# A decoder layer in one core: the projections after q, k, v with activations instead of weights as the stationary operand

## The chip, the core and the metric

One core of a Trainium2 chip runs the whole layer in one launch. TensorE (PE) multiplies matrices and writes to PSUM; VectorE (DVE), ScalarE (ACT) and GpSimd (POOL) work on tiles; SyncE (SP) issues DMAs. The metric is the device time in microseconds of the core. The kernel before takes 1522.69 us (median of three runs, 1522.31 to 1523.57).

## The reference

For 256 tokens of width 2048, in float32, with P the weights' columns of each part:

```
u = rmsnorm(x)
q,k,v,z | beta,decay | qb,kb,vb | gate_a,gate_b = u @ w_in
y_a = gated_deltanet(conv(q,k,v), z, beta, decay)     # 8 heads of 128
y_b = block attention(qb, kb, vb)                     # 8 heads of 128
mix = sigmoid(gate_a) * (y_a @ w_gdn) + sigmoid(gate_b) * (y_b @ w_moba)
h   = x + mix @ w_out
u   = rmsnorm(h)
out = h + (silu(u @ w_gate) * (u @ w_up)) @ w_down    # w_gate, w_up: 2048 x 5632
```

## The kernel before, in words

All weights stand in DRAM in the order of their use as 504 units of 128 partitions x 1024 float32 (512 KB). Each is split into `whi` (rounded to the matmul's fp32r type, by ACT, L67) and `wlo` (the rest, by DVE, L68). Activations are kept split in the same way, as a high part of 256 tokens and a low part of 256 tokens in one row of 512. A product is the sum hi*hi + hi*lo + lo*hi, in one of two forms:

- `fm_jobs` (feature-major, L149): a 128x128 piece of the weights is the stationary operand. `whi` meets all 512 columns of the activations (L169), `wlo` the 256 high ones (L170). A unit is 8 such pairs, 16 matmuls with 6144 moving columns in all. The output stands features x tokens, in two halves that have to be added (`evac`, ACT L279 and DVE L280).
- `tm_job` (token-major): a 128x128 piece of the activations is stationary, and 512 columns of weights move past it: high x `whi` (L189), high x `wlo` (L190), low x `whi` (L191). A unit is 4 such triples, 12 matmuls with 6144 moving columns as well. The output stands tokens x features in one piece.

Units 0 to 111 are q, k, v of the convolution (fm), z and qb, kb, vb (tm). The other 392 units are all fm before the change: gates and branches 96, w_out 32, gate and up 176, down 88.

`Weights.get` runs through the units: it asks for loads ahead (DMAs on SP's queue, 1 MB chunks of two units, three buffers), splits up to three units ahead into four buffers, and hands one unit to PE. The small work of the attention parts is a set of generators (`chains`), of which a job advances one step every so many matmuls (`tick`); what is put into `late` runs whole at the next tick. Instructions then stand on each engine's queue in an order that the tile framework chooses and are executed in that order; an instruction waits for its operands by semaphores, and what stands behind it waits too. Two PSUM tiles of two banks (`mm`) hold the jobs' sums, four single banks (`aux`) all else.

At the start `x_part` (L230) loads x in four chunks and the first weights, and two fm jobs run together. In g = 0 of the first attention part a 16x16 solve loads `lb` (1 MB, broadcast out of a DRAM scratch, issued by ACT) and works on it on DVE (L485, L486).

Of the kernel before, what the change touches and what calls it, by code (L numbers as in the profile page):

```python
# [16 lines left out]
P = 128  # L17
# [16 lines left out]
SPLIT_AHEAD = 3  # L34
TICK = 8


class Weights:
# [3 lines left out]
    def __init__(self, nc, pool, src):  # L42
        self.nc, self.pool, self.src = nc, pool, src
        self.n = 2 * src.shape[0]
        self.raw, self.parts = {}, {}

    def load(self, c):
        if c in self.raw or 2 * c >= self.n:
            return
        t, src = self.pool.tile([P, 2, 1024], F32, name="wraw", tag="wraw", bufs=3), self.src[c]  # L50
        if c == 0:
            self.first = [lambda: self.nc.sync.dma_start(t[:, 0, :512], src[:, 0, :512]),
                          lambda: self.nc.sync.dma_start(t[:, 0, 512:], src[:, 0, 512:]),
                          lambda: self.nc.sync.dma_start(t[:, 1], src[:, 1])]
# [25 lines left out]
def layer(ctx: ExitStack, tc: tile.TileContext, xT, xtok, params, consts, relt, w_bd, w, out):  # L80
# [35 lines left out]
    warm = small("warm", [2])  # L116
    nc.scalar.activation(warm, ones[:, :2], AF.Tanh)

# [30 lines left out]
    def fm_jobs(act, nk, m, before=None, apart=False):  # L149

        get = act if callable(act) else lambda kc: act[:, kc]
        if apart:
            pss = [[aux.tile([P, 512], F32, name="psh", tag="aux") for _ in range(2)]]
            halves = pss
        else:
            pss = [mm.tile([P, 2, 512], F32, name="ps", tag="mm") for _ in range(m)]
            halves = [[ps[:, j] for j in range(2)] for ps in pss]
        for k0 in range(0, nk, 4):  # L160
            if before:
                before(k0)
            for ps in halves:
                hi, lo = W.get(cursor[0])
                cursor[0] += 1
                for j in range(2):
                    for kc in range(k0, k0 + 4):
                        sl = slice((kc % 4) * 256 + j * P, (kc % 4) * 256 + (j + 1) * P)
                        nc.tensor.matmul(ps[j], hi[:, sl], get(kc), start=kc == 0, stop=False)  # L169
                        nc.tensor.matmul(ps[j][:, :T], lo[:, sl], get(kc)[:, :T], start=False, stop=kc == nk - 1)  # L170
# [7 lines left out]
    def tm_job(act, nk):  # L178

        ps = mm.tile([P, NT, 512], F32, name="ps", tag="mm")  # L180
        for kc in range(nk):
# [4 lines left out]
            for n in range(NT):  # L186
                ah = act[:, kc, n * P:(n + 1) * P]
                al = act[:, kc, T + n * P:T + (n + 1) * P]
# [7 lines left out]
    def token_scale(name, ssq, rows=None):  # L196


        rb, r = small(name + "b", [T]), small(name, [NT])

        def steps():
            total = ssq
            if rows is not None:
                with tc.issue_after(W.last_hi.ins):
                    for n in range(NT):
                        nc.scalar.activation(rows[:, n], rows[:, n], AF.Square, accum_out=ssq[:, n:n + 1])
            else:
                p = aux.tile([P, 512], F32, name="pss", tag="aux")
                for n in range(NT):
                    nc.tensor.matmul(p[:, 2 * n:2 * n + 2], ssq[:, n * P:(n + 1) * P], ones[:, :2], start=True,  # L210
                                     stop=True)
                total = p[:, :2 * NT].rearrange("p (n j) -> p n j", j=2)[:, :, 0]
            nc.vector.tensor_copy(r, rsqrt(name + "r", total, 1.0 / DM))
            yield
            p2 = aux.tile([P, 512], F32, name="pbc", tag="aux")
            for n in range(NT):
                nc.tensor.transpose(p2[:, n * P:(n + 1) * P], r[:, n:n + 1].to_broadcast([P, P]), ident)
            nc.vector.tensor_copy(rb, p2[:, :T])

        return r, rb, steps()  # L220
# [3 lines left out]
    rsum = small("xssq", [NT])  # L224
    xrow = acts.tile([P, NT, DM], F32, name="xrow", tag="actB")
    with tc.tile_pool(name="xin", bufs=4) as xin:
        xcs = {}

        def x_part(k0):
            xc = xcs[k0] = xin.tile([P, 4, T], F32, name="xc", tag="xc")  # L230
            W.load(k0 // 4)
            if k0 == 0:
                for i in range(2):
                    W.first[i]()
                    nc.sync.dma_start(xc[:, 2 * i:2 * i + 2], xT[:, 2 * i:2 * i + 2])
                W.first[2]()
            else:
                nc.sync.dma_start(xc, xT[:, k0:k0 + 4])
            if k0 == 4:
                nc.sync.dma_start(ident, consts[:, :P])  # L240
            if k0 == 8:
                nc.sync.dma_start(par, params)
            if k0 == KM - 4:
                nc.sync.dma_start(xrow, xtok)
            for k in range(4):
                kc = k0 + k
                nc.scalar.activation(aT[:, kc, :T], xc[:, k], AF.Copy, scale=wmix[:, kc:kc + 1])
                nc.vector.scalar_tensor_tensor(aT[:, kc, T:], xc[:, k], wmix[:, kc:kc + 1],  # L248
# [123 lines left out]
    def gdn_project(g):  # L372
# [8 lines left out]
        held = [evac(ps, "cu", md, "md", 6) for ps in first] if g == 0 else []  # L381
        for i in range(len(held), len(dsts)):
            u = evac(fm_job(aT, KM), "cu", md, "md", 6)
            if held:
                drain(1)
                nc.vector.tensor_scalar(r1h, r1, 0.5, None, op0=ALU.mult)
# [334 lines left out]
    def gated(yT, dst):  # L721
        s = evac(fm_job(aT, KM), "gt", md, "md", 6)
        nc.gpsimd.tensor_mul(s, s, bcm(r1b, 2))
        nc.scalar.activation(s, s, AF.Tanh, scale=0.5)
        b = evac(fm_job(yT, H), "br", md, "md", 6)
        nc.vector.scalar_tensor_tensor(dst, s, 1.0, b, op0=ALU.add, op1=ALU.mult)
# [4 lines left out]
    for j in range(KM // 2):  # L731
        m = s2.tile([P, 2, T], F32, name="mix", tag="t2", bufs=14)
        gated(yaT, m)
        mix.append(m)
# [5 lines left out]
    for j in range(KM // 2):  # L740
        m = md.tile([P, 2, T], F32, name="mixb", tag="md", bufs=6)
        gated(ybT, m)
        nc.gpsimd.tensor_add(m, m, mix[j])
        hi = mixT[:, 2 * j:2 * j + 2, :T]
        nc.scalar.activation(hi, m, AF.Copy, scale=0.5)
        nc.vector.scalar_tensor_tensor(mixT[:, 2 * j:2 * j + 2, T:], m, 0.5, hi.bitcast(F32),
                                       op0=ALU.mult, op1=ALU.subtract)


    hT = acts.tile([P, KM, T], F32, name="hT", tag="actB")  # L750
    uT = acts.tile([P, KM, 512], F32R, name="uT", tag="actA")
    hsq = small("hsq", [T])
    for j in range(KM // 2):
        xr = md.tile([P, 2, T], F32, name="xr", tag="md", bufs=6)
        nc.sync.dma_start(xr, xT[:, 2 * j:2 * j + 2])
        ps = fm_job(mixT, KM)
        hj = hT[:, 2 * j:2 * j + 2]
        nc.vector.tensor_add(hj, ps[:, :, T:], xr)
        nc.vector.tensor_add(hj, ps[:, :, :T], hj)
        for i in range(2):  # L760
            kc = 2 * j + i
            nc.scalar.activation(uT[:, kc, :T], hT[:, kc], AF.Copy, scale=wffn[:, kc:kc + 1])
            nc.vector.scalar_tensor_tensor(uT[:, kc, T:], hT[:, kc], wffn[:, kc:kc + 1],
                                           uT[:, kc, :T].bitcast(F32), op0=ALU.mult, op1=ALU.subtract)
        sq = md.tile([P, 2, T], F32, name="hq", tag="md", bufs=6)
        nc.scalar.activation(sq, hj, AF.Square)
        if j == 0:
            nc.gpsimd.tensor_add(hsq, sq[:, 0], sq[:, 1])
        else:
            nc.gpsimd.tensor_add(sq[:, 0], sq[:, 0], sq[:, 1])  # L770
            nc.gpsimd.tensor_add(hsq, hsq, sq[:, 0])
    low_stage.close()
    mid.close()
    r2, r2b, scale_steps = token_scale("r2", hsq)
    r2bh = small("r2bh", [T])
    chains.append(scale_steps)
# [134 lines left out]
```

## Time and profile before

| | |
|---|---|
| median of three runs | 1522.69 us |
| the profiled execution | 1520.97 us |
| its span, first to last instruction | 1519.2 us |
| granted TensorE clock, mean | 0.999 |
| PE busy | 1496.4 us (99%) |
| DVE, ACT, POOL busy | 937.1, 712.3, 161.7 us |
| DMA | 277.95 MB, 183 GB/s on average |

Times in the rows are microseconds from the start of the span, unless marked ns. A matmul's own duration overlaps that of its neighbours; what a stream of them costs is the distance from start to start. L numbers are lines of the kernel. PEld is PE's loading of stationary operands, which runs beside the matmuls.

### The profile page before, as it was taken

The numbers are of one execution on the slowest core, as the hardware profiler recorded it, in microseconds if no ns is written. First come the engines' busy times: TensorE is split into PE (matmuls) and PEld (weight loads), VectorE is DVE, ScalarE is ACT, GpSimd is POOL, SyncE is SP. The second block draws the span as 40 slices with busy tenths as digits, with TensorE's granted clock in tenths as the row PEclk, the third lists the DMA queues.
The fourth block names the chain that finished last, engine by engine and source line by source line (L and its number), as shares of the span: only waits on it lengthen the run. The fifth ranks groups of instructions, "written<-read, shape, count | busy, mean of one in ns | idle before, by whom it ended". The sixth has DMA issues, their size and how long they took to land.

```text
span 1519.2 us, 21248 instructions
## 1 busy us (share of the span) xinstructions
PE 1496.4 (99%) x8586; PEld 1291.0 (85%) x8586; DVE 937.1 (62%) x1231; ACT 712.3 (47%) x1008; POOL 161.7 (11%) x125
## 2 busy tenths in 40 slices
PE   7999899999999999999999999999999999999999
PEld 5888778887888888888888888888888888888887
DVE  5878867866775566666665555555555655444443
ACT  5644445445454444554544444444444444333332
POOL 0003002301100111111221111111111110000000
PEclk9999999999999999999999999999999999999999
DMA  8453634643435555556655555555455555555552
GB/s 322 167 198 137 194 112 166 181 182 112 181 129 191 194 195 189 185 186 219 220 188 177 190 194 181 182 192 190 177 189 194 182 181 192 199 190 193 201 190 80
DMA packets 41841, 277.95 MB, mean 183 GB/s; under 512 B 4752, under 2 KB 5648, under 8 KB 9232
## 3 DMA queue, kind: packets, MB, share of 16 engines
q1 hardware_dynamic: 41040, 274.25, 50.9%
q10 hardware_dynamic: 704, 2.36, 0.7%
q8 instruction: 67, 1.10, 0.3%
q14 instruction: 30, 0.25, 0.0%
HBM read 274.36 MB, written 2.23 MB: 182 GB/s over the span
## 4 chain that ended last, share of the span: by engine, by line
PE 91%; DVE 4%; DMA 2%; ACT 1%; POOL 1%; issue 1%; SPq 0%; ACTq 0%; POOLq 0%
PE ps L169 49%; PE ps L170 25%; PE ps L189 4%; PE ps L191 4%; PE ps L190 3%; DMA wraw<-in_w 2%; PE psh L169 1%; DVE wlo L68 1%; DVE cacc L365 1%; PE psh L170 1%; ACT whi L67 0%; PE pO L699 0%; PE pU L566 0%; PE pO L574 0%; PE pb L296 0%
## 5 line engine op out<-in xcount | busy, mean ns | idle before, releaser
L68 DVE TENSOR_TENSOR wlo<-wraw,whi 128x1024 fp32r<-128x1024 f32 (+1 forms) x505 | 639.5, 1268 | 449.7 <-ACT whi L67 449.0
L67 ACT CAST whi<-wraw 128x1024 fp32r<-128x1024 f32 (+1 forms) x505 | 528.3, 1049 | 632.9 <-PE ps L169 518.6
L169 PE MATMUL ps<-uT,whi 128*128 128x512 f32 x1408 | 497.7, 399 | 0.0
L170 PE MATMUL ps<-uT,wlo 128*128 128x256 f32 x1408 | 395.4, 281 | 0.0
L169 PE MATMUL ps<-aT,whi 128*128 128x512 f32 x896 | 319.2, 398 | 9.7 <-DVE aT L248 7.9
L169 PEld LDWEIGHTS ps<-uT,whi 128*128 128x128 f32 x1408 | 264.5, 188 | 66.0
L170 PEld LDWEIGHTS ps<-uT,wlo 128*128 128x128 f32 x1408 | 266.0, 189 | 0.0
L170 PE MATMUL ps<-aT,wlo 128*128 128x256 f32 x896 | 253.7, 283 | 7.5 <-DVE wlo L68 7.4
L169 PEld LDWEIGHTS ps<-aT,whi 128*128 128x128 f32 x896 | 169.5, 189 | 48.7 <-DVE aT L248 8.9
L170 PEld LDWEIGHTS ps<-aT,wlo 128*128 128x128 f32 x896 | 171.0, 191 | 9.8 <-DVE wlo L68 9.6
L169 PE MATMUL ps<-high,whi 128*128 128x512 f32 x504 | 178.4, 399 | 0.0
L170 PE MATMUL ps<-high,wlo 128*128 128x256 f32 x504 | 141.6, 281 | 0.0
L169 PEld LDWEIGHTS ps<-high,whi 128*128 128x128 f32 x504 | 94.7, 188 | 23.6
L189 PE MATMUL ps<-whi,aT 128*128 128x512 f32 x256 | 102.0, 398 | 0.0
L191 PE MATMUL ps<-whi,aT 128*128 128x512 f32 x256 | 101.2, 395 | 0.0
L190 PE MATMUL ps<-wlo,aT 128*128 128x512 f32 x256 | 100.5, 392 | 0.0
L170 PEld LDWEIGHTS ps<-high,wlo 128*128 128x128 f32 x504 | 95.2, 189 | 0.0
L169 PE MATMUL ps<-mixT,whi 128*128 128x512 f32 x256 | 88.8, 391 | 0.0
L170 PE MATMUL ps<-mixT,wlo 128*128 128x256 f32 x256 | 71.7, 280 | 0.0
L169 PEld LDWEIGHTS ps<-mixT,whi 128*128 128x128 f32 x256 | 47.9, 187 | 10.5
L191 PEld LDWEIGHTS ps<-whi,aT 128*128 128x128 f32 x256 | 48.1, 188 | 9.7
L190 PEld LDWEIGHTS ps<-wlo,aT 128*128 128x128 f32 x256 | 48.1, 188 | 9.2
(335 smaller groups left out, 1456.2 us busy)
## 6 DMA issues: line engine op xcount, KB each, us to landing
wraw<-in_w SPq DMA_DIRECT2D x251, 1024.0 KB, 4.8
xrow<-in_xtok SPq DMA_DIRECT2D x1, 2048.0 KB, 13.8
lb<-dm ACTq DMA_DIRECT2D x2, 1024.0 KB
xr<-in_xT SPq DMA_DIRECT2D x8, 256.0 KB, 5.3
out<-fo SPq DMA_DIRECT2D x7, 256.0 KB, 2.8
xc<-in_xT SPq DMA_DIRECT2D x3, 512.0 KB, 10.9
bias<-in_relt SPq DMA_DIRECT2D x4, 256.0 KB, 5.1
wraw<-in_w SPq DMA_DIRECT2D x2, 256.0 KB, 3.9
```

The costliest lines, as they stand in the source:

```text
L67: self.last_hi = self.nc.scalar.copy(hi[:, f], raw[:, f])
L68: self.last_lo = self.nc.vector.tensor_sub(lo[:, f], raw[:, f], hi[:, f].bitcast(F32))
L169: nc.tensor.matmul(ps[j], hi[:, sl], get(kc), start=kc == 0, stop=False)
L170: nc.tensor.matmul(ps[j][:, :T], lo[:, sl], get(kc)[:, :T], start=False, stop=kc == nk - 1)
L189: nc.tensor.matmul(ps[:, n], ah, hi[:, sl], start=kc == 0, stop=False)
L190: nc.tensor.matmul(ps[:, n], ah, lo[:, sl], start=False, stop=False)
L191: nc.tensor.matmul(ps[:, n], al, hi[:, sl], start=False, stop=kc == nk - 1)
L365: nc.vector.scalar_tensor_tensor(acc[:, j, d:], u[:, j, :T - d], w[:, 3 - d:4 - d], acc[:, j, d:], op0=ALU.mult, op1=ALU.add)
```

## The change

The 392 units after qb, kb, vb become `tm_job`s; `gated`, the w_out loop and the FFN loops are written anew for token-major outputs. Norm factors are then per partition, so they go into the activation's scale or a scalar operand, and the POOL multiplications by a broadcast row go. Where the next product needs the result as its stationary operand (the mix, h, and the FFN's hidden values), PE turns it: `turn` puts four 128x128 transposes into an `aux` bank and ACT and DVE split them from there. Two turns (one per 128 tokens) run at the first tick of the next job, after 24 of its matmuls; there are 4 pairs for the mix, 4 for h and 11 for the hidden values. The sum of squares of h comes from ACT's accumulation by rows, not from a matmul with ones (`pss`) and a broadcast by PE (`pbc` of r2). Output is written token-major, through POOL's queue but for the last two.

Weights are loaded by single units into seven buffers. At the start x goes through ACT's queue beside SP's weights, the table load stands behind these DMA issues, the 2 MB row copy of x (`xrow`) is asked for after the first two jobs, and the evacuation of the first two jobs is put behind the splits already issued.

```diff
 class Weights:
...
-    def load(self, c):
-        if c in self.raw or 2 * c >= self.n:
+    def load(self, u, cuts=1):
+        if u in self.raw or u >= self.n:
             return
...
+        t = self.raw[u] = self.pool.tile([P, 1024], F32, name="wraw", tag="wraw", bufs=RAW)
+        for i in range(cuts):
+            f = slice(i * 1024 // cuts, (i + 1) * 1024 // cuts)
+            self.nc.sync.dma_start(t[:, f], self.src[u, :, f])
...
     def get(self, u):
-        for k in range(u // 2, u // 2 + 2):
+        for k in range(u, u + RAW - 1):
             self.load(k)
...
+    def turn(src, evict):
 
         def steps():
...
+            p = aux.tile([P, 4, P], F32, name="pT", tag="aux")
+            for i in range(4):
+                nc.tensor.transpose(p[:, i], src[:, i * P:(i + 1) * P], ident)
+            evict(p)
+        late.append(steps)
...
+        for i in range(2):
+            nc.scalar.dma_start(xcs[0][:, 2 * i:2 * i + 2], xT[:, 2 * i:2 * i + 2])
+        W.load(0, 2)
+        for c in range(1, KM // 4):
+            nc.scalar.dma_start(xcs[c], xT[:, 4 * c:4 * c + 4])
+        for u in range(1, RAW):
+            W.load(u)
...
-        held = [evac(ps, "cu", md, "md", 6) for ps in first] if g == 0 else []
+        held = []
+        if g == 0:
+            with tc.issue_after(W.last_hi.ins), tc.issue_after(W.last_lo.ins):
+                held = [evac(ps, "cu", md, "md", 6) for ps in first]
...
+    def gated(yT, name, dst):
+        pg = tm_job(aT, KM)
+        gate = []
+        for n in range(NT):
+            s = mdt("gt")
+            nc.scalar.activation(s, pg[:, n], AF.Tanh, scale=r1h[:, n:n + 1])
+            gate.append(s)
+        pb = tm_job(yT, H)
+        for n in range(NT):
+            d = dst(name)
+            nc.vector.scalar_tensor_tensor(d, gate[n], 1.0, pb[:, n], op0=ALU.add, op1=ALU.mult)
+            yield n, d
...
+    for j in range(4):
+        for n, m in gated(ybT, "mixb", mdt):
+            nc.vector.tensor_add(m, m, mix[j][n])
+            turn(m, halved(j, n))
...
+        ps = tm_job(mixT, KM)
+        for n in range(NT):
+            nc.vector.tensor_add(h[:, n, fs], ps[:, n], xr[n])
+            nc.scalar.activation(xr[n], h[:, n, fs], AF.Square, accum_out=hss[:, n, j:j + 1])
+            turn(h[:, n, fs], weighted(j, n))
...
+    for c in range(KF // 4):
+        pg = tm_job(uT, KM)
...
+            nc.scalar.activation(g, pg[:, n], AF.Tanh, scale=r2h[:, n:n + 1])
+            nc.vector.scalar_tensor_tensor(g, g, 1.0, pg[:, n], op0=ALU.add, op1=ALU.mult)
+            gs.append(g)
+        pu = tm_job(uT, KM)
+        for n in range(NT):
+            nc.vector.scalar_tensor_tensor(gs[n], pu[:, n], r2q[:, n:n + 1], gs[n], op0=ALU.mult, op1=ALU.mult)
+            turn(gs[n], parted(c, n))
+    for j in range(4):
+        ps = tm_job(hid, KF)
+        for n, dma in enumerate((nc.gpsimd, nc.gpsimd) if j < 3 else (nc.sync, nc.scalar)):
+            s = fft("fo")
+            nc.vector.tensor_add(s, ps[:, n], h[:, n, 512 * j:512 * j + 512])
+            dma.dma_start(out[:, n, 512 * j:512 * j + 512], s)
```

The changed kernel's `h_scale` (13 small DVE instructions on 128x2 values, at a tick of the first FFN job) stands in place of `token_scale` for r2. How the change stands in three places of the engines' orders:

PE in the first FFN jobs, before: the end of the first gate job (`ps_6845`), the broadcast of r2 (`pbc`), and the start of the first up job.

```order
L169 MATMUL ps_6845<-uT_6057,whi_6868 128x512
L170 MATMUL ps_6845<-uT_6057,wlo_6869 128x256
L217 MATMUL pbc_6949<-ident_77,r2_6838 128x128 x2
L169 MATMUL ps_6961<-uT_6057,whi_6909 128x512
L170 MATMUL ps_6961<-uT_6057,wlo_6910 128x256
```

PE in the FFN now: 24 matmuls into a gate job (`ps_7173`), the two turns of the chunk before (`fg_7020`, `fg_7023`), and on.

```order
L177 MATMUL ps_7173<-whi_7155,uT_5802 128x512
L178 MATMUL ps_7173<-wlo_7156,uT_5802 128x512
L179 MATMUL ps_7173<-whi_7155,uT_5802 128x512
L189 MATMUL pT_7210<-ident_75,fg_7020 128x128 x4
L189 MATMUL pT_7217<-ident_75,fg_7023 128x128 x4
L177 MATMUL ps_7173<-whi_7176,uT_5802 128x512
L178 MATMUL ps_7173<-wlo_7177,uT_5802 128x512
L179 MATMUL ps_7173<-whi_7176,uT_5802 128x512
```

Pairs of 512 and 256 columns have become triples of 512, and eight transposes of 128 columns stand in the stream once a chunk.

DVE in the FFN, before: one gate and up pair of 256 features (`fgl_7138`, `ful_7230`) with the splits between.

```order
L280 TENSOR_TENSOR fgl_7138<-ps_7053,fgl_7138 128x512
L68 TENSOR_TENSOR wlo_7191<-wraw_7188,whi_7190 128x1024
L795 SCALAR_TENSOR_TENSOR fgl_7138<-fth_7142,fgl_7138 128x512
L68 TENSOR_TENSOR wlo_7211<-wraw_7188,whi_7210 128x1024
L68 TENSOR_TENSOR wlo_7241<-wraw_7238,whi_7240 128x1024
L68 TENSOR_TENSOR wlo_7261<-wraw_7238,whi_7260 128x1024
L280 TENSOR_TENSOR ful_7230<-ps_7145,ful_7230 128x512
L798 TENSOR_TENSOR fgl_7138<-fgl_7138,ful_7230 128x512
L68 TENSOR_TENSOR wlo_7283<-wraw_7280,whi_7282 128x1024
L801 TENSOR_TENSOR low_6843<-fgl_7138,low_6843 128x2x256
```

DVE in the FFN now: the end of an up job (`ps_7026`), of 512 features, up to the split of the turned values (`pT_7210`, `pT_7217`).

```order
L65 TENSOR_TENSOR wlo_7177<-wraw_7117,whi_7176 128x1024
L816 SCALAR_TENSOR_TENSOR fg_7020<-ps_7026,r2q_6512,fg_7020 128x512
L816 SCALAR_TENSOR_TENSOR fg_7023<-ps_7026,r2q_6512,fg_7023 128x512
L65 TENSOR_TENSOR wlo_7195<-wraw_7135,whi_7194 128x1024
L65 TENSOR_TENSOR wlo_7227<-wraw_7153,whi_7226 128x1024
L65 TENSOR_TENSOR wlo_7245<-wraw_7174,whi_7244 128x1024
L801 TENSOR_TENSOR low_6516<-pT_7210,low_6516 128x4x128
L801 TENSOR_TENSOR low_6516<-pT_7217,low_6516 128x4x128
```

What the turns wait for (L816, twice) stands ahead of the next splits; the halves' additions (L280) are gone.

ACT at the end of the first two jobs, before, with the evacuations (`cul`) and the row copy's squares (`xrow`).

```order
L67 CAST whi<-wraw 128x1024 x2
L247 ACTIVATE aT<-xc,wmix 128x256 x4
L279 COPY cul<-ps 128x512 x2
L67 CAST whi<-wraw 128x1024 x4
L206 ACTIVATE xrow,xssq<-xrow 128x2048 x2
```

ACT in the same place now.

```order
L215 ACTIVATE aT<-xc,wmix 128x256 x4
L64 CAST whi<-wraw 128x1024
L318 ACTIVATE expa<-par 128x8
L64 CAST whi<-wraw 128x1024 x4
L262 COPY cul<-ps 128x512
L64 CAST whi<-wraw 128x1024
L262 COPY cul<-ps 128x512
L228 ACTIVATE xrow,xss<-xrow 128x2048 x2
```

The first `cul` has moved behind four splits, the second behind a fifth.

## Rows read from the trace of the kernel before

**Rows 1.** The page: span, engines, and the chain that ended last.

```profile
span 1519.2 us, 21248 instructions
PE 1496.4 (99%) x8586; PEld 1291.0 (85%) x8586; DVE 937.1 (62%) x1231; ACT 712.3 (47%) x1008; POOL 161.7 (11%) x125
PE 91%; DVE 4%; DMA 2%; ACT 1%; POOL 1%; issue 1%; SPq 0%; ACTq 0%; POOLq 0%
```

**Rows 2.** Windows: us, busy (x) of PE, PEld, DVE, ACT, POOL, PEclk, DMA share, GB/s.

```profile
12.00:20.00 8.00, 6.75 (x38) 5.44 (x37) 6.40 (x9) 6.79 (x12) 0.00 (x0) 1.00 1.03 417
...
116.00:256.00 140.00, 132.79 (x827) 111.02 (x826) 108.06 (x199) 64.75 (x129) 21.47 (x15) 0.99 0.45 146
...
781.00:1266.00 485.00, 485.00 (x2748) 420.50 (x2747) 281.02 (x280) 227.26 (x258) 55.60 (x43) 1.00 0.52 186
1267.00:1484.00 217.00, 217.00 (x1230) 188.24 (x1230) 103.82 (x92) 81.45 (x79) 1.29 (x1) 1.00 0.54 192
```

**Rows 3.** Line L169 on PE, two stages: count, durations, first and last start.

```profile
L169 PE MATMUL ps<-mixT,whi x255: 391/391/391, 679.2 to 767.2; 128*128 128x512 f32 x128
...
L169 PE MATMUL ps<-uT,whi x1375: 395/398/403, 780.6 to 1266.1; 128*128 128x512 f32 x197
```

**Rows 4.** PE's timeline around 24 token-major triples (start, us, line, operation).

```profile
290.30 0.48 PE L189 MATMUL ps<-whi,aT 128*128 128x512 f32 x1
290.62 0.40 PE L190 MATMUL ps<-wlo,aT 128*128 128x512 f32 x1
...
306.72 1.03 PE L495 MATMUL pv<-ident,v 128*128 128x128 f32 x8
307.51 0.48 PE L189 MATMUL ps<-whi,aT 128*128 128x512 f32 x1
307.83 0.40 PE L190 MATMUL ps<-wlo,aT 128*128 128x512 f32 x1
```

**Rows 5.** PE's timeline at the norm factor r2.

```profile
773.87 0.61 PE L210 MATMUL pss<-ones,hsq 128*128 128x2 f32 x4 [0.22 <-POOL hsq L771]
774.33 0.48 PE L169 MATMUL ps<-uT,whi 128*128 128x512 f32 x1
```

**Rows 6.** PE's timeline at the end of the first two jobs.

```profile
33.42 0.28 PE L170 MATMUL ps<-aT,wlo 128*128 128x256 f32 x1
35.32 0.50 PE L169 MATMUL ps<-aT,whi 128*128 128x512 f32 x1 [1.62 <-ACT whi L67]
36.58 0.39 PE L170 MATMUL ps<-aT,wlo 128*128 128x256 f32 x1 [0.76 <-DVE wlo L68]
```

**Rows 7.** ACT's timeline before unit 2.

```profile
12.59 2.00 ACT L67 CAST whi<-wraw 128x1024 fp32r<-128x1024 f32 x2 [1.49 <-DMA wraw<-in_w]
14.49 1.70 ACT L247 ACTIVATE aT<-xc,wmix 128x256 fp32r<-128x256 f32 x4
```

**Rows 8.** PE's timeline at unit 2.

```profile
16.48 0.50 PE L169 MATMUL ps<-aT,whi 128*128 128x512 f32 x1 [1.25 <-DVE aT L248]
```

**Rows 9.** Waits from 140 to 200: us in total, times, longest.

```profile
ACT whi L67 <- DMA wraw<-in_w: 6.9, 2, 5.4
PE ps L170 <- DVE wlo L68: 6.7, 4, 4.0
...
DVE prod L485 <- DMA lb<-dm: 4.0, 1, 4.0
```

**Rows 10.** Groups of instructions on DVE: busy us, mean ns of one, idle before.

```profile
L68 DVE TENSOR_TENSOR wlo<-wraw,whi 128x1024 fp32r<-128x1024 f32 (+1 forms) x505 | 639.5, 1268 | 449.7 <-ACT whi L67 449.0
...
L795 DVE SCALAR_TENSOR_TENSOR fgl<-fth,fgl 128x512 f32<-128x512 f32 x22 | 14.9, 678 | 0.0
```

**Rows 11.** DMA issues: count, KB of one, median us to landing.

```profile
wraw<-in_w SPq DMA_DIRECT2D x251, 1024.0 KB, 4.8
...
out<-fo SPq DMA_DIRECT2D x7, 256.0 KB, 2.8
...
out<-fl ACTq DMA_DIRECT2D x1, 128.0 KB, 1.8
```

**Rows 12.** DVE's timeline at the end.

```profile
1515.87 0.42 DVE L813 TENSOR_TENSOR fl<-psh,fl 128x256 f32<-128x256 f32 x1
```

More of the change, by code (lines that the diff above doesn't have):

```diff
@@ L34 @@
 SPLIT_AHEAD = 3
+RAW = 7
 TICK = 8
@@ L147, in drain, with fm_jobs @@
             tick()
[L149 to L159, printed above, removed]
+    def fm_jobs(act, nk, m, before=None):
+        pss = [mm.tile([P, 2, 512], F32, name="ps", tag="mm") for _ in range(m)]
         for k0 in range(0, nk, 4):
@@ L194, in tm_job @@
         return ps
-    def token_scale(name, ssq, rows=None):
-        rb, r = small(name + "b", [T]), small(name, [NT])
+    def turn(src, evict):
         def steps():
[L202 to L220, printed above, removed]
+            p = aux.tile([P, 4, P], F32, name="pT", tag="aux")
[3 more added lines that the diff above has]
+        late.append(steps)
@@ L222, in layer @@
     ident = small("ident", [P])
     aT = acts.tile([P, KM, 512], F32R, name="aT", tag="actA")
-    rsum = small("xssq", [NT])
     xrow = acts.tile([P, NT, DM], F32, name="xrow", tag="actB")
     with tc.tile_pool(name="xin", bufs=4) as xin:
-        xcs = {}
-        def x_part(k0):
[L230 to L244, printed above, removed]
+        xcs = [xin.tile([P, 4, T], F32, name="xc", tag="xc") for _ in range(KM // 4)]
@@ new lines, in layer @@
+        for i in range(2):
[5 more added lines that the diff above has]
+            W.load(u)
+            if u == 4:
+                nc.sync.dma_start(ident, consts[:, :P])
+                nc.sync.dma_start(par, params)
+        warm = small("warm", [2])
+        nc.scalar.activation(warm, ones[:, :2], AF.Tanh)
@@ L730, in layer @@
         tick()
[L731 to L734, printed above, removed]
+    for j in range(4):
+        mix.append([m for _, m in gated(yaT, "mix", lambda name: s2.tile([P, 512], F32, name=name, tag="t2", bufs=14))])
     drain()
@@ L739, in layer @@
     mixT = mx.tile([P, KM, 512], F32R, name="mixT")
[L740 to L750, printed above, removed]
@@ L751, in layer, with halved, evict @@
-    uT = acts.tile([P, KM, 512], F32R, name="uT", tag="actA")
[L752 to L771, printed above, removed]
+    def halved(j, n):
+        def evict(p):
+            hi = mixT[:, 4 * j:4 * j + 4, n * P:(n + 1) * P]
+            nc.scalar.activation(hi, p, AF.Copy, scale=0.5)
+            nc.vector.scalar_tensor_tensor(mixT[:, 4 * j:4 * j + 4, T + n * P:T + (n + 1) * P], p, 0.5,
+                                           hi.bitcast(F32), op0=ALU.mult, op1=ALU.subtract)
+        return evict
@@ new lines, in layer, with weighted, evict @@
+    for j in range(4):
+        for n, m in gated(ybT, "mixb", mdt):
+            nc.vector.tensor_add(m, m, mix[j][n])
+            turn(m, halved(j, n))
+    h = acts.tile([P, NT, DM], F32, name="h", tag="actB")
+    uT = acts.tile([P, KM, 512], F32R, name="uT", tag="actA")
+    hss = small("hss", [NT, 4])
+    def weighted(j, n):
+        def evict(p):
+            for i in range(4):
+                kc = 4 * j + i
+                hi = uT[:, kc, n * P:(n + 1) * P]
+                nc.scalar.activation(hi, p[:, i], AF.Copy, scale=wffn[:, kc:kc + 1])
+                nc.vector.scalar_tensor_tensor(uT[:, kc, T + n * P:T + (n + 1) * P], p[:, i], wffn[:, kc:kc + 1],
+                                               hi.bitcast(F32), op0=ALU.mult, op1=ALU.subtract)
+        return evict
@@ L802, in layer, with fft @@
[L802 to L814 removed]
+    def fft(name):
+        return ff.tile([P, 512], F32, name=name, tag="ff", bufs=4)
@@ L817, in _bucket @@
+    for j in range(4):
+        ps = tm_job(hid, KF)
[3 more added lines that the diff above has]
+            dma.dma_start(out[:, n, 512 * j:512 * j + 512], s)
 def _bucket():
```

122 lines of the change are left out of this document (57 added, 65 removed).

## The prediction

> **What bounds the kernel now.** I read the page first: PE is busy for 1496.4 of 1519.2 us and has 91% of the chain that ended last [rows 1]; a reader should see that no other engine holds the end for long. Busy time of overlapping matmuls does not say how fast they go, so the windows by stage came next: from 781 to 1484 PE is busy in every microsecond, while DVE is busy for 281.02 of 485 us and the DMA engines for 0.52 to 0.54 of their time [rows 2]. There the time is the number of matmuls times their distance, and the distance is what the change alters. So I took it from first and last starts by line, and from the one stretch where the token-major form runs undisturbed. Last I read the places where PE does stand still, in the first 260 us: 132.79 busy of 140 us between 116 and 256 [rows 2], and two waits at 33 to 37 [rows 6].
>
> **The two forms.** A feature-major unit is 8 pairs. In the w_out stage 255 pairs start between 679.2 and 767.2, 0.3465 us apart; in gate and up 1375 start between 780.6 and 1266.1, 0.3533 apart [rows 3]; the down stage gives the same (217 us for 615 pairs, 0.3528) [rows 2]. Gates, branches and w_out (128 units) I take at 0.3465, gate, up and down (264 units) at 0.3533: 128 x 8 x 0.3465 + 264 x 8 x 0.3533 = 354.8 + 746.2 = 1101.0 us.
>
> A token-major unit is 4 triples. From 290.30 to 306.72 stand 72 matmuls, 24 triples, of which the first matmul took 0.32 to its successor instead of 0.23 because transposes precede it [rows 4]: (16.42 - 0.09) / 24 = 0.6804 us, so 392 x 4 x 0.6804 = 1066.9 us. **Gain 34.1 us.** Both forms move 6144 columns a unit; what is saved is what each instruction costs beyond its columns, on 12 instructions instead of 16.
>
> This spacing has been seen only before 390 us. The feature-major pair has two values, 6.8 ns apart, each held over hundreds of pairs, with the granted clock at 1.00 throughout [rows 2, 3]. A triple could jump by as much: 1568 triples x 6.8 ns = 10.7 us either way, which I keep for the range.
>
> By the Trainium skill (TensorE: Matmul & The Clock Gate, Back-to-back issue gap) a warm matmul of N columns takes about N/2.4 + 2.5 ns: 325.0 ns for a pair and 647.5 ns for a triple, so that the gain would be only about 4 us. The trace disagrees with both figures (346.5 or 353.3, and 680.4), and the measurement decides.
>
> **The turns.** 19 pairs of turns, 8 transposes of 128x128 each. The same thing stands at 306.72: eight transposes last until 307.51, and the next matmul costs 0.09 more [rows 4]. 0.79 + 0.09 = 0.88, 19 x 0.88 = **16.7 us lost**. Bounds: 15.0 without the after-effect, 21.7 if eight took their whole 1.03 us and the after-effect. All of it is on the path, as PE has no idle time there. What PE could wait for in addition is DVE: in the FFN two operations of 0.68 us [rows 10] after the up job, for the mix four (2.7 us), and they stand ahead of the next split in DVE's order. PE comes to the transposes 24 matmuls, 5.4 us, after the job's end, so 2.7 us are left in the tightest place. ACT and DVE also split the turned values, beside PE, in less DVE time than the additions that go.
>
> **Small terms.** The sum of h's squares by matmul goes: 773.87 to 774.33, with the after-effect and the broadcast of r2 **0.8 us gained** [rows 5]. POOL's multiplications go from beside PE: nothing.
>
> **The first 40 us.** Before, ACT does two evacuations before it splits unit 8; PE loses 1.62 and 0.76 [rows 6]. With four splits ahead of the first evacuation that goes. What is late next is the PSUM tile: job 2 may write only after the first evacuation (ACT 0.6, DVE 0.7 behind a split of 1.27), some 0.2 us after unit 7. Gain 2.2. On the other side weights and x now arrive by two queues. The DMA engines are saturated there, 417 GB/s at a share of 1.03 [rows 2]. Before, the chunk with unit 3 had landed at 12.59 [rows 7], as the last of 2.6 MB (0.5 of x, 2.1 of weights); if the two queues share equally, it now is the last of 4.2 MB (all 2.1 of x beside it), and 1.6 MB more at 417 GB/s are 3.8 us. As `whi` of units 1 to 3 still stands ahead of `aT` of chunk 1 in ACT's order, unit 2, which began at 16.48 [rows 8], would begin at about 19.2: ACT's split at 16.4, aT at 17.4, DVE's aT after its split at 18.7. Loss 2.7. Everything later has its data in time, x being there already. Bounds for the sum: 2.4 gained to 3.8 lost; I take **0.5 lost**.
>
> **The solve at 150 to 183.** DVE waits 4.0 us for `lb`, ACT 5.4 for weights behind the same DMAs, and PE at last 4.0 for a split [rows 9]. The order there is nearly the same. Splits are freed as before, but seven buffers of one unit hold six or seven units landed where three of two hold four or five, about 1.5 units, 4 us more cover; DVE's wait for `lb` stays. Of PE's 6.7 us I take **2 back**; bounds: the 7.2 us idle of the window [rows 2] gained, and 4 lost by one more such wait.
>
> **Weights in small loads.** 512 KB in 2.72 us is 193 GB/s, under half of the 417 that queued loads reach [rows 2]; a load asked for seven units ahead has 15 us and more, where a twice as large one lands in 4.8 [rows 11]. Cost nothing.
>
> The Trainium skill's rule speaks against it (DMA: Bandwidth & Descriptors, Bandwidth: batch DMAs to at least 1 MiB), and by its 2.0 us plus bytes/436e3 one such load after the other would take 3.2 us a unit, an estimate of 190 us more. That holds for loads that do not overlap; the trace's 417 GB/s comes from loads that do.
>
> **The end.** Before, two additions (0.42 the last, [rows 12]) and 128 KB, 1.8 us; now one addition of 0.69 and 256 KB, which in mid-stream land in 2.8 [rows 11]. Between equal and 0.8 more: **0.4 lost**.
>
> **Sum.** -34.1 + 16.7 - 0.8 + 0.5 - 2 + 0.4 = -19.3. The profiled execution took 1520.97 us (1519.2 of span and 1.8 around it); the median is 1.7 above it. 1522.69 - 19.3 = 1503.4, and with the sum's own roundings I say 1503.
>
> **Rivals.**
> 1. The gain and PE's early idle time go together: all 7.2 us between 116 and 256 vanish, and the first 40 us gain 2.2. Time 1495. For it: the waits there hang on DMA arrival; against: DVE's order is unchanged.
> 2. Slower: the token-major stream holds a longer distance in the late stages, one 6.8 ns step per matmul instead of per triple, 392 x 12 x 6.8 ns = 32 us. Time 1535. It decides from 12 ns per triple, the net gain over 1568 triples. For it: the pair's two values without a visible cause; against: triples were alike wherever they ran.
> 3. Turns wait: one more split of 1.27 us stands before what they need, 19 x 1.27 = 24 us, 1527. Against: DVE's order as shown, and 2.7 us of margin. From 1 us a pair it eats all.
> 4. Columns alone set the time in both forms, 6144 a unit each: no gain in the matmuls, the turns remain, 1538. Against: the distances measured. The skill's gap formula (page above) comes close to this.
> 5. Weights come late because single units do not overlap: the change doesn't hold its stream; far above 1523. Against: DMA at half its time.
>
> **Chances.** Forecast 0.80 (its own range 1497 to 1510), rival 1 0.08, rivals 2 to 5 0.03, 0.04, 0.02, 0.02, the remainder anything. With the jump of 10.7 us either way and the bounds of the first 260 us the range is 1493 to 1512. A measurement of this kernel tells 0.2%, 3 us, from no change. Faster: forecast, rival 1 and the milder half of rival 3, 0.92; within 0.2%: 0.03; slower 0.05.
>
> **What would show it.** Token-major triples 0.680 us apart in all late stages; eight transposes in 0.8 us without idle time of PE before them; no wait of PE for `whi` at 33; unit 2 beginning near 19; the late stages, from the first gate unit, 18 us shorter. Wrong would be: triples over 0.69, PE waiting for DVE at the turns, or PE waiting for splits in the FFN.

## The result and the profile after

The changed kernel takes 1499.87 us (median of four runs, 1498.37 to 1501.35) against 1522.56 of before beside it (1522.31 to 1523.57): a ratio of 0.985, 95% interval 0.9833 to 0.9867. 1503 had been predicted, with 1493 to 1512 as the range. The profiled execution took 1498.37 us, 1496.6 of span, 22.6 less than before.

The page after: span, engines, and the chain that ended last, which answer to [rows 1].

```profile
span 1496.6 us, 18724 instructions
PE 1474.1 (98%) x7164; PEld 1227.0 (82%) x7164; DVE 868.9 (58%) x1161; ACT 675.8 (45%) x956; POOL 56.7 (4%) x48
PE 91%; DVE 4%; DMA 2%; ACT 1%; issue 1%; POOL 0%; SPq 0%; DVEq 0%; ACTq 0%; POOLq 0%
```

PE still has 91% of the chain. The same windows as in [rows 2], in their columns:

```profile
12.00:20.00 8.00, 8.00 (x40) 6.70 (x39) 6.39 (x9) 6.10 (x12) 0.00 (x0) 1.00 1.04 403
116.00:256.00 140.00, 135.08 (x854) 113.53 (x853) 109.91 (x202) 68.67 (x144) 22.44 (x16) 1.00 0.52 152
775.00:1260.00 485.00, 485.00 (x2187) 402.67 (x2186) 255.94 (x242) 208.17 (x220) 0.00 (x0) 1.00 0.64 190
1262.00:1478.00 216.00, 216.00 (x954) 178.92 (x953) 101.49 (x86) 83.35 (x79) 3.41 (x6) 1.00 0.64 191
```

In the FFN PE is busy throughout, as before, with 2187 matmuls in 485 us instead of 2748. To see where 22.6 us went, I cut both spans at matmuls that are the same in both, named by the PSUM tile that they are the first to write: `pgr` is the 541st matmul in either kernel, `pv` the 853rd, `pD` the 957th. The first late unit is unit 112, the first of the 392 that the change turns into `tm_job`s; from there to the last matmul is the late part.

| stretch | before | after | difference | forecast |
|---|---|---|---|---|
| start to `pgr` | 114.09 | 112.07 | -2.0 | +0.5 |
| `pgr` to `pv` | 53.50 | 53.24 | -0.3 | 0 |
| `pv` to `pD` (the solve) | 25.25 | 21.29 | -4.0 | -2 |
| `pD` to the first late unit | 203.13 | 203.24 | +0.1 | 0 |
| first late unit to the last matmul | 1119.12 | 1101.80 | -17.3 | -18.2 |
| last matmul's start to the end | 4.1 | 4.9 | +0.9 | +0.4 |

Each column is one execution. The late part repeats closely (1119.12 and 1119.13 before, 1101.80 and 1101.94 after, from the runs `before_again` and `after_again` below); the first two hundred us do not. In the five traces with the changed kernel's start `pgr` stands at 111.79 to 112.52, in the four with the start of before at 113.13 to 114.09, which is 1.4 on average instead of 2.0. `pv` to `pD` takes 21.2 to 22.5 in eight traces with the new loads and 25.2 to 26.7 in four of before, 4.1 on average.

PE's timeline at the first turns (answers to [rows 4]):

```profile
576.82 0.39 PE L178 MATMUL ps<-wlo,aT 128*128 128x512 f32 x1
577.04 0.39 PE L179 MATMUL ps<-whi,aT 128*128 128x512 f32 x1
577.27 1.03 PE L189 MATMUL pT<-ident,mixb 128*128 128x128 f32 x8
578.07 0.47 PE L177 MATMUL ps<-whi,aT 128*128 128x512 f32 x1
578.38 0.40 PE L178 MATMUL ps<-wlo,aT 128*128 128x512 f32 x1
```

Matmuls start 0.227 apart, three in 0.680; the eight transposes follow without a gap and take 0.80, and the next matmul 0.31. Over all 19 pairs of turns one pair costs 0.889 us, 0.88 had been said.

PE's timeline at its first matmul and at unit 2 (answers to [rows 8]):

```profile
10.20 0.79 PE L156 MATMUL ps<-aT,whi 128*128 128x512 f32 x1 [10.20 <-DVE aT L216]
10.79 0.41 PE L157 MATMUL ps<-aT,wlo 128*128 128x256 f32 x1
11.01 0.63 PE L156 MATMUL ps<-aT,whi 128*128 128x512 f32 x1
11.43 0.41 PE L157 MATMUL ps<-aT,wlo 128*128 128x256 f32 x1
11.64 0.63 PE L156 MATMUL ps<-aT,whi 128*128 128x512 f32 x1
...
17.77 0.46 PE L156 MATMUL ps<-aT,whi 128*128 128x512 f32 x1
...
34.51 0.27 PE L157 MATMUL ps<-aT,wlo 128*128 128x256 f32 x1
34.89 0.50 PE L156 MATMUL ps<-aT,whi 128*128 128x512 f32 x1
```

PE begins 3.5 us later than before, but then runs without a wait; unit 2 is 1.3 late, not 2.7. At 34.51 stands what was 1.62 and 0.76 of waiting in [rows 6]: 0.38 instead of 0.12 from start to start.

Waits from 140 to 200 (answers to [rows 9]):

```profile
PE ps L157 <- DVE wlo L65: 3.1, 3, 1.5
ACT whi L64 <- DMA wraw<-in_w: 2.4, 1, 2.4
DVE prod L470 <- DMA lb<-dm: 2.0, 1, 2.0
```

All three have fallen to half or less in this execution; in `after_again` they are 4.2, 3.6 and 3.2. A wait that nobody forecast stands in the block attention: first the waits from 385 to 465, then PE's timeline there.

```profile
DVE sc L662 <- DMA bias<-in_relt: 4.2, 2, 2.2
```

```profile
411.49 0.39 PE L178 MATMUL ps<-wlo,aT 128*128 128x512 f32 x1
412.75 0.61 PE L681 MATMUL pPT<-ident,sc 128*128 128x128 f32 x3 [0.87 <-DVE sc L672]
```

From 411.49 to 412.75 pass 1.26 us where a matmul costs 0.23; at 443 it is 1.36. Together they lose 2.2 us.

DMA issues (answers to [rows 11]), and DVE's timeline at the end (answers to [rows 12]):

```profile
wraw<-in_w SPq DMA_DIRECT2D x503, 512.0 KB, 4.0
```

```profile
1492.07 1.29 DVE L822 TENSOR_TENSOR fo<-ps,h 128x512 f32<-128x512 f32 x2 [8.57 <-PE ps L179]
```

The two last additions run one behind the other on DVE, 1.29 us, where the estimate had a single one of 0.69.

### The profile page after: what moved, and what is told of

Same layout as the page of the kernel before. It is cut to its first block, busy times and chain, and to the rows that moved or that the text cites. A ratio compares the mean times of both kernels' runs of the same rounds, so it can differ in the third digit from the quotient of the medians.

```text
span 1496.6 us, 18724 instructions
## 1 busy us (share of the span) xinstructions
PE 1474.1 (98%) x7164; PEld 1227.0 (82%) x7164; DVE 868.9 (58%) x1161; ACT 675.8 (45%) x956; POOL 56.7 (4%) x48
## 4 chain that ended last, share of the span: by engine, by line
PE 91%; DVE 4%; DMA 2%; ACT 1%; issue 1%; POOL 0%; SPq 0%; DVEq 0%; ACTq 0%; POOLq 0%
PE ps L179 27%; PE ps L177 27%; PE ps L178 27%; PE ps L156 3%; PE ps L157 2%; PE pT L189 1%; DVE wlo L65 1%; DMA lb<-dm 1%; DMA bias<-in_relt 1%; DVE cacc L348 1%; DMA wraw<-in_w 0%; ACT whi L64 0%; PE pU L551 0%; PE pO L559 0%; PE pb L279 0%
## 5 line engine op out<-in xcount | busy, mean ns | idle before, releaser
L177 PE MATMUL ps<-whi,uT 128*128 128x512 f32 x704 | 274.8, 390 | 0.0
L179 PE MATMUL ps<-whi,uT 128*128 128x512 f32 x704 | 273.9, 389 | 0.0
L178 PE MATMUL ps<-wlo,uT 128*128 128x512 f32 x704 | 273.9, 389 | 0.0
L177 PE MATMUL ps<-whi,aT 128*128 128x512 f32 x512 | 202.8, 396 | 0.0
L179 PE MATMUL ps<-whi,aT 128*128 128x512 f32 x512 | 201.3, 393 | 0.0
L179 PEld LDWEIGHTS ps<-whi,uT 128*128 128x128 f32 x704 | 132.2, 188 | 27.5
L177 PEld LDWEIGHTS ps<-whi,uT 128*128 128x128 f32 x704 | 132.2, 188 | 27.0
L178 PEld LDWEIGHTS ps<-wlo,uT 128*128 128x128 f32 x704 | 132.2, 188 | 27.0
L156 PE MATMUL ps<-aT,whi 128*128 128x512 f32 x384 | 137.6, 401 | 10.3 <-DVE aT L216 10.2
L179 PEld LDWEIGHTS ps<-whi,aT 128*128 128x128 f32 x512 | 96.2, 188 | 19.7
L177 PE MATMUL ps<-whi,high 128*128 128x512 f32 x288 | 112.0, 389 | 0.0
L178 PE MATMUL ps<-wlo,high 128*128 128x512 f32 x288 | 112.0, 389 | 0.0
L179 PE MATMUL ps<-whi,high 128*128 128x512 f32 x288 | 112.0, 389 | 0.0
L157 PE MATMUL ps<-aT,wlo 128*128 128x256 f32 x384 | 108.6, 283 | 3.1 <-DVE wlo L65 3.1
L178 PEld LDWEIGHTS ps<-wlo,aT 128*128 128x128 f32 x512 | 96.3, 188 | 18.7
L177 PEld LDWEIGHTS ps<-whi,aT 128*128 128x128 f32 x512 | 96.3, 188 | 18.4
L156 PEld LDWEIGHTS ps<-aT,whi 128*128 128x128 f32 x384 | 73.0, 190 | 27.4 <-DVE aT L216 10.2
## 6 DMA issues: line engine op xcount, KB each, us to landing
xrow<-in_xtok SPq DMA_DIRECT2D x1, 2048.0 KB, 10.2
```

Of the source, the lines that this page charges most:

```text
L156: nc.tensor.matmul(ps[:, j], hi[:, sl], act[:, kc], start=kc == 0, stop=False)
L157: nc.tensor.matmul(ps[:, j, :T], lo[:, sl], act[:, kc, :T], start=False, stop=kc == nk - 1)
L177: nc.tensor.matmul(ps[:, n], ah, hi[:, sl], start=kc == 0, stop=False)
L178: nc.tensor.matmul(ps[:, n], ah, lo[:, sl], start=False, stop=False)
L179: nc.tensor.matmul(ps[:, n], al, hi[:, sl], start=False, stop=kc == nk - 1)
```

## The experiments

**1. Each turn twice.** In `turn`: `for i in range(8)` and `p[:, i % 4]`, `src[:, i % 4 * P:...]`.

> The changed kernel with each turn's four transposes issued twice into the same bank, the same result. If the turns lie wholly on PE's path, as the prediction has it, the 19 pairs cost 19 x 0.79 = 15.0 us once more, up to 16.7 with the after-effect: 1515 to 1517 us, and each group of transposes at 0.79 us now lasts 1.6. Rival: part of a turn fills time in which PE would have waited anyway (for splits or a PSUM tile), then clearly less than 15 us, 0 if all of it.

Measured: 1515.73 us (1514.94 to 1516.16, ten runs), 16 above the changed kernel's medians on other chips. The late part took 1118.86, 17.1 more. PE's timeline:

```profile
577.86 1.91 PE L189 MATMUL pT<-ident,mixb 128*128 128x128 f32 x16
579.52 0.47 PE L177 MATMUL ps<-whi,aT 128*128 128x512 f32 x1
```

Sixteen take 1.66 instead of 0.80: a turn costs its full price, and nothing of it fills idle time. On this chip, where experiments 1 to 4 ran, the kernel before spread widely beside it (23 runs, 1507.0 to 1528.8), this variant of the changed one by 1.2 us; see 10.

**2. Token-major matmuls in halves.** The late units' three matmuls become

```
for a, wt, first, end in ((ah, hi, ...), (ah, lo, ...), (al, hi, ...)):
    for c in range(0, 512, 256):
        nc.tensor.matmul(ps[:, n, c:c + 256], a, wt[:, sl.start + c:sl.start + c + 256], ...)
```

> The changed kernel with every matmul of the 392 late units cut into two of 256 columns: 24 a unit instead of 12, the same columns, the same sums. Theory: an instruction costs its columns and a fixed 13 ns (680 - 640 = 40 ns per triple). 12 more a unit x 392 x 13.4 ns = +63 us, or +34 us if 256 columns take 0.117, the distance from wlo's matmul to its successor in the feature-major pair: 1534 to 1563 us. Rival 1: columns alone set the time, the forms differ for another reason: 0, 1500 us. Rival 2: a matmul of 256 columns waits for the loading of its stationary operand (188 ns on PEld): 24 x 0.188 = 4.5 us a unit, +700 us.

Measured: 1561.1 us (two runs); the late part 1164.44, 62.6 more. PE's timeline in the FFN:

```profile
899.74 0.64 PE L180 MATMUL ps<-whi,uT 128*128 128x256 f32 x4
900.22 0.40 PE L180 MATMUL ps<-wlo,uT 128*128 128x256 f32 x2
900.46 0.64 PE L180 MATMUL ps<-whi,uT 128*128 128x256 f32 x4
```

Six start within 0.720, 120.0 ns each: 62.6 us / 4704 added instructions = 13.3 ns. So 256 columns cost 106.7 + 13.3 and 512 cost 213.3 + 13.3 = 226.7. Neither columns alone nor the 188 ns of a load on PEld set it. The Trainium skill (TensorE: Matmul & The Clock Gate, Back-to-back issue gap) has 2.5 ns beside the columns, for a matmul taken by itself; by an estimate from that, this would have been 12 us. These runs give five times that.

**3. Feature-major in thirds.** In the kernel before, `whi`'s matmul in the late units as two of 256 columns.

> The kernel before with the 512-column matmul of whi in the 392 late units cut into two of 256: three matmuls of 256 columns a piece instead of 512 + 256. Theory of a fixed cost per instruction: 3136 pieces x 13.4 ns = +42 us, or between -7 and +14 if each takes 0.117 (0.351 a piece against 0.3465 and 0.3533): 1516 to 1565 us. Rival 1: columns alone, 0. Rival 2: each of three is bound by the 188 ns load of its operand: 0.564 a piece, +660 us. The 6.8 ns between the pair's two values: if it belongs to the pattern of unequal lengths, equal lengths show one value in all stages; if to the stage, two values remain.

Measured: 1550.07 us (two runs), 29 above the median beside it; late part 1146.87, 27.8 more. PE's timeline:

```profile
900.16 0.40 PE L171 MATMUL ps<-uT,whi 128*128 128x256 f32 x2
900.40 0.28 PE L173 MATMUL ps<-uT,wlo 128*128 128x256 f32 x1
900.52 0.40 PE L171 MATMUL ps<-uT,whi 128*128 128x256 f32 x2
```

Three in 0.360 from 460 to the end, in every stage: equal lengths hold one value. A pair should then cost 226.7 + 120.0 = 346.7, which is the lower of the two values; the extra 6.7 at the upper one (20 ns in three pairs) is something else. 1024 pairs x 13.3 + 2112 x 6.7 = 27.8, as measured.

**4. Single-unit loads in the kernel before.** 512 KB each, six buffers.

> The kernel before with weights loaded by single units of 512 KB into six buffers (as many bytes as its three of 1 MB), all else as it was. Theory: it is the loads that shorten the stretch with the solve, where the changed kernel gained 3.9 us between pv at 167.6 and pD at 192.8: -2 to -4 us, and PE's wait of 4.0 us for a split gone or halved. Rival 1: the gain there came of the order of the splits or of x's row copy being asked for later: 0 within 0.5 us. Rival 2: small loads cost, as a rule of at least 1 MiB would have it: slower by more than 10 us.

Measured: 1521.58 us (1509.30 to 1523.62) against 1521.22 (1507.0 to 1528.8), ratio 1.0004 (0.997 to 1.0039): the whole doesn't tell it, the trace does. `pv` to `pD` took 23.22, 2.0 less than in [rows 9]'s kernel. Waits from 140 to 200:

```profile
PE ps L170 <- DVE wlo L68: 5.3, 3, 3.4
...
DVE prod L486 <- DMA lb<-dm: 2.4, 1, 2.4
```

PE's stalls at 33 to 37 are gone here as well, but unit 2 starts at 18.8, 2.4 later, so nothing is won by `pgr` (113.81). And the small loads have a price: the late part takes 1121.31, 2.2 more than before. DVE waits for the bias here too, as in the changed kernel and not in the kernel before; waits from 385 to 465, then PE's timeline:

```profile
DVE sc L678 <- DMA bias<-in_relt: 3.8, 2, 2.0
```

```profile
415.33 0.40 PE L169 MATMUL ps<-aT,whi 128*128 128x512 f32 x1
416.86 0.61 PE L697 MATMUL pPT<-ident,sc 128*128 128x128 f32 x3 [1.13 <-DVE sc L688]
```

What the loads win in the solve they lose there, which is why the whole shows nothing.

**5. Pairs of units in the changed kernel.** 1 MB, three buffers.

> The changed kernel with loads of 1 MB (two units) and three buffers as before, all else as changed. Theory, as the kernel before with single units lost 2.0 us less between pv and pD than with pairs (25.2 to 23.2): the loads are half of the 3.9 us gained in that stretch, so pv to pD is 23.3 here instead of 21.3, PE's wait for a split there over 3 us, and the whole +2 us (1502). Rival 1: the order around it (x's row copy asked for later, evacuations behind the splits) carries the stretch alone: 21.3 again, 1500. Rival 2: all of it hangs on the loads: 25.2, +4 us.

Measured: 1502.40 us (1501.85 to 1503.48). `pv` to `pD` 26.08, and the old wait is back. Waits from 140 to 200:

```profile
PE ps L162 <- DVE wlo L70: 6.5, 4, 4.0
...
DVE prod L475 <- DMA lb<-dm: 4.0, 1, 4.0
```

The second rival was right for the stretch: in the changed kernel all of it hangs on the loads, of which size (512 KB or 1 MB) and room (seven units or six) change together here. In experiment 4, with room for six, they alone brought 2.0 us, 2.7 against the mean of before. The whole loses only 2.5 to 2.9 us, since the wait for the bias isn't there with these loads: the late part is 1099.74, 2.1 less.

**6. x on SP's queue again.** x's chunks between the first weights' loads on `nc.sync`.

> The changed kernel with x on SP's queue between the first weights, as before, instead of on ACT's queue. Prediction's term: the second queue brings the weights of unit 3 later, which costs 1.3 us by the trace of the changed kernel (unit 2 at 17.8 against 16.5). If one queue in order of need is better, PE begins near 7 instead of 10.2, unit 2 near 16.5, and everything to the first transposes pt comes 1.3 us earlier: 1498.5. Rival: the bytes needed decide (DMA at its limit of some 417 GB/s), PE begins earlier but waits later, pt within 0.5 us of 55.6: 1500. Rival 2: the second queue was the better one, since PE runs without a gap once it has begun: pt later by over 0.5 us.

Measured: 1498.81 us (1497.74 to 1500.34). PE begins at 6.37, waits in between, and reaches unit 2 at 16.07 and `pgr` at 111.53, 0.5 earlier. `pt`, the first transposes, is 1.4 later, but 18 matmuls more stand before it, so it was a bad mark. With experiment 9's `best`, which has this edit too (111.06), `pgr` is 0.8 earlier on average than in the five traces with the second queue: it did cost, less than the 1.3 expected. The medians don't tell so small a difference.

**7. Evacuations not put behind the splits.** Without the two `issue_after`.

> The changed kernel without the rule that puts the first two jobs' evacuation behind the splits already issued. Prediction's term: two stalls of 1.62 and 0.76 us at 33 to 37 come back: PE waits for whi and wlo there again, pt 2.2 us later (57.8), 1502. Rival: with weights there in time (seven units landed instead of two or three chunks), the stalls stay away, since it was the loads and not ACT's order that made ACT late: pt at 55.6, 1500.

Measured: 1499.94 us (1499.29 to 1500.57), `pgr` at 111.81, no stall. ACT's timeline:

```profile
31.63 1.05 ACT L64 CAST whi<-wraw 128x1024 fp32r<-128x1024 f32 x1 [1.72 <-PE ps L156]
32.58 0.58 ACT L262 COPY cul<-ps 128x512 f32<-128x512 f32 x1
```

Splits stand ahead of the first evacuation without any rule. The rival was right: with single-unit loads the rule is not needed. Experiment 5 has the rule and 1 MB loads, and PE doesn't stall there either: neither is needed beside the other.

**8. The bias on POOL's queue.** `nc.gpsimd.dma_start(bias, ...)`.

> The changed kernel with the four loads of the block attention's bias on POOL's queue instead of SP's, where they stand behind weights. In the changed kernel DVE waits twice for them, 4.2 us in all, between 385 and 465, and PE stands still for 1.26 us at 411 and 1.36 at 443, ahead of the transposes of the probabilities. Theory: these 2.6 us come from the load's place in SP's queue and go: 1497 to 1498. Rival: the chain behind the load (two reductions, two exponentials) or the splits are the next thing late, and PE stands still all the same: 1500.

Measured: 1497.65 us (1496.85 to 1499.12); late part 1099.48, 2.3 less. PE's timeline, now without a wait before the probabilities:

```profile
413.76 0.39 PE L177 MATMUL ps<-whi,aT 128*128 128x512 f32 x1
413.99 0.27 PE L681 MATMUL pPT<-ident,sc 128*128 128x128 f32 x1
```

It isn't a slower load: from issue to landing the bias took 4.1 us after and 5.1 before (medians). It is when the load is issued and when it is needed. On SP's queue the second of the four stands behind a weight load and is issued at 405.21; on POOL's queue it goes out with the first, from 383.40 on. And PE comes to these transposes 7.7 us after the scores instead of 10.2, because the framework's order has only 20 other matmuls between them where it had 46. That order goes with the loads and not with the form of the matmuls: experiment 5, token-major with 1 MB loads, has 35 matmuls, 10.1 us and no wait, experiment 4, feature-major with single units, 26 matmuls, 8.1 us and the wait. Timelines of SP in the changed kernel and of POOL here:

```profile
404.78 0.33 SPq L54 DMA_DIRECT2D wraw<-in_w  x1
405.21 0.37 SPq L653 DMA_DIRECT2D bias<-in_relt  x1
```

```profile
383.40 1.26 POOL L653 DMA_DIRECT2D bias<-in_relt  x2
```

**9. The changed kernel again, and both edits that helped.** Experiments 6 and 8 in one kernel.

> The changed kernel unchanged, beside the next one on the same chip: 1500 within 1.5 us, and PE waiting again twice for some 1.3 us ahead of the transposes of the probabilities (411 and 443).

> The changed kernel with both edits that made single places better: the bias on POOL's queue (2.3 us less between pqT and the end) and x on SP's queue in order of need (pgr 0.5 us earlier). If the two add, 2.3 to 2.8 us less than the changed kernel on the same chip: 1497. Rival: with x back on SP's queue the solve or the bias's successors wait more, and the sum is 0 to 1 us.

Measured on one chip: 1499.48 us (1499.42 to 1500.14) and 1497.66 us (1495.74 to 1498.42), four runs each that do not overlap, 1.8 apart where 2.3 had been expected at least; against the kernel before 0.9858 (0.9841 to 0.9874) and 0.9844 (0.9829 to 0.9859). `pgr` is 1.5 earlier and the late part 1099.54 against 1101.94. The median is that of experiment 8 alone (1497.65, on another chip).

**10. What sets the pair's value.** The kernel before with two transposes of `ident` ahead of every late job, and the kernel before once more.

> The kernel before with two transposes of ident (result unused) ahead of each of the 91 late feature-major jobs but the last. Theory: the pair's distance is drawn anew wherever PE's stream is broken, and then held: jobs at 346.7 and jobs at 353.3 ns a pair stand mixed in every stage, gates as well as FFN. The breaks cost 91 x 0.22 = 20 us (two transposes 0.14 at 780.07, the next matmul 0.08 more), so 1522 + 20 with as much at either value as before, 1528 to 1549 at the ends (all at 346.7, all at 353.3). Rival: the value belongs to the stage (operand, address, DMA load): gates and w_out all at 346.7 and FFN all at 353.3 again.

> The kernel before unchanged. On one chip its 23 runs lay at 1507 to 1509 (6), 1511 to 1513 (2), 1519 to 1524 (9) and 1527 to 1529 (6). Theory: what differs is at which of the pair's two values each stage runs (6.7 ns x 2112 pairs of the FFN = 14 us, x 1024 pairs of gates and w_out = 7 us): near 1508 the whole is at 346.7, near 1522 the FFN alone at 353.3, near 1529 all. The time of this execution and the distances in its trace have to agree with that. Rival: the times differ by something else (waits early on), and the distances are as in the first profile whatever the time.

(The 23 runs are 5, 2, 10 and 6 in the four groups, not 6, 2, 9 and 6.) Measured: 1534.47 us (1531.86 to 1540.92), the profiled execution at 1540.92; and 1521.19 for the kernel before. The breaks cost 19.8 us in the late part, 20 had been said. L169 of the first, by stage (durations min/median/max, first and last start):

```profile
L169 PE MATMUL ps<-uT,whi x1408: 391/398/481, 777.2 to 1284.5; 128*128 128x512 f32 x176
...
L169 PE MATMUL ps<-mixT,whi x256: 391/391/476, 686.6 to 776.7; 128*128 128x512 f32 x128
```

A duration of 391 belongs to 346.7 a pair, the cycle 395, 398, 403 to 353.3 [rows 3]. In spite of 91 breaks w_out stood almost wholly at the lower value and the FFN at the upper: for the rival. But the stage doesn't fix it either. This is the same stretch, 36 to 44.5, in two executions of the changed kernel, the first profile and `after_again`:

```profile
L156 PE MATMUL ps<-aT,whi x26: 391/391/391, 35.7 to 44.4; 128*128 128x512 f32 x26
```

```profile
L156 PE MATMUL ps<-aT,whi x25: 395/398/403, 36.0 to 44.4; 128*128 128x512 f32 x25
```

One program, one stretch, both values. The second kernel, `before_again`, fell among the runs near 1521 and has the distances of the first profile, so it decides nothing. What sets the value stays open; that the runs at 1507 to 1509 and 1527 to 1529 are those with all stages at the lower or the upper one fits in size (14 and 7 us), but none of them has a trace.

## Why the prediction was right, and where it was not

**The two forms: right in sum, not in reason.** 392 x 4 x 0.680 = 1066.2; against the forecast's 1101.0 this is a gain of 34.8, where 34.1 had been said. The text called all of it what instructions cost beyond their columns. By experiments 2 and 3 that is 4 fewer instructions x 392 x 13.3 ns = 20.9 us. The other 14 are the FFN's 2112 pairs at 353.3 instead of 346.7, which the triples, of equal lengths, don't have. The sum held because both distances were measured, and because the kernel before stood at the same value beside the changed one; that is luck. Against an execution of before at 346.7 throughout, the gain would be some 9 us (22.7 - 14), an estimate. On experiment 1's chip 5 of its 23 runs took 1507.0 to 1508.8; the changed kernel itself wasn't run there. The forecast's jump of 10.7 us for triples never came; where a turn disturbs the stream, a few matmuls are some ns longer and it settles at once.

**The turns: right**, 19 x 0.889 = 16.9 against 16.7, all on the path (experiment 1), with no wait for DVE or a split: rivals 3 and 4 are out, and rival 2 with the 0.680. (The upper bound of 21.7 should have been 19 x 1.12 = 21.3.)

**The late part's missing term: the bias.** 34.8 - 16.9 + 0.8 = 18.7 would have gone; 17.3 did. The new wait of 2.2 (experiment 8) takes it back and more; the remaining 0.8 in the other direction I have not traced. The prediction looked for late waits in the turns and the FFN's splits, and gave the small loads no price. They have one, 2.1 us (experiment 5) and 2.2 (experiment 4): not in their own arrival, but in a small load on the same queue and in what the framework's order makes of it.

**The first 40 us: wrong by 2.5** in this execution, by 1.9 on the average of the traces. "Loss 2.7" for unit 2 was 1.3 (1.5 on average): equal sharing of the two queues was too pessimistic, since ACT could split unit 3 at 14.97 instead of 16.4. "Gain 2.2" for the stalls was right in size, and ACT's order, splits ahead of evacuations, is as said; but the loads bring that order without the rule (experiment 7). Besides, PE's pairs from 19 to 45 stood at 346.7 where in the trace before they stood at 353.3, some 75 pairs, 0.5 us. That is luck: `after_again` has the upper value there (experiment 10), and its `pgr` is 0.45 later.

**The solve: direction right, half the size.** 4.0 instead of 2. The cause was named rightly, more units landed: between the issue of `lb` and its landing ACT splits five units instead of four, and without the new loads the stretch is at 26.1 again (experiment 5). What failed is "DVE's wait for `lb` stays": the same 1 MB broadcast was waited for 2.0 us instead of 4.0, 2.0 to 3.2 in all eight traces with the new loads, 2.4 in experiment 4, and 4.0 again in experiment 5. So this wait goes with the size of the weight loads beside it; why the broadcast lands sooner then is not shown.

**Weights in small loads: right for their own stream**; a load lands in 4.0 us, and PE never waits for one in the FFN. "Cost nothing" is not right beside the bias, as said above. The Trainium skill's minimum of 1 MiB (DMA: Bandwidth & Descriptors, Bandwidth) is for 75% of the peak; the FFN here moves 190 GB/s where 417 were seen, so no run tests that rule. (The prediction's 2.0 us plus bytes/436e3 is, on the same page of the Trainium skill, a fit for loads issued by GpSimd; here SP issues them.) At this rate 512 KB instead of 1 MB shortened the solve by 2.0 us (experiment 4) and 4.8 (experiment 5, on the means 2.7 and 4.2). Rival 5 is out, and rival 1 held in part: of 7.2 us of idle time from 116 to 256 now 4.9 are left (windows).

**The end**: +0.9 for +0.4, two additions in a row instead of one.

By term, in the two profiled executions, the errors were -0.7 (forms), +0.2 (turns), +2.2 (bias), -0.8 (not traced), -2.5 (head), -0.3 (to `pv`), -2.0 (solve), +0.1 and +0.5 (end): -3.3 in all, the 22.6 measured against 19.3. That the unforeseen bias and the too small gains early on partly cancel is luck too.

## What to carry to other kernels

Price a matmul form by instructions as well as columns: here 120.0 ns for 256 columns and 226.7 for 512 in an even stream, N/2.4 + 13.3, so the form with fewer and longer matmuls gains as long as its turns cost less. A stream of unequal lengths can hold two distances; look for both before a saving is put down to the form. When the loads of a big stream are cut smaller, look again at every small load on the same queue and at where the framework now puts what needs it.

## What the runs showed of the hardware that was not expected

- The upper value of the pair is a cycle of three pairs, 361 + 349 + 350 ns, 20 ns longer than three times 346.7, held for up to 700 us; one program shows both values in the same stretch (experiment 10).
- The first pairs after PE's start at 10.20 take 0.64 us: 0.42 and 0.21 (from 11.01 in the rows above), which is what 512 and 256 columns take at 1.2 GHz (427 and 213 ns), while the granted clock reads 1.00; PE had been idle until then, and from 14.6 on a pair takes 0.347. Begun at 6.37 with waits in between (experiment 6), the long pairs last until 13.6.
- Transposes of 128 columns in a run follow each other at 0.109 us, where 128 columns at 2.4 GHz, which the matmuls around them hold, would take 0.053.
